# State space stage of a hybrid decoder step: loads one step in front, and keys, values and masks kept in DRAM meanwhile

## The chip, the cores and the metric

One core of a Trainium2 chip runs the whole step in one launch. The metric is the device time of an execution in microseconds; the kernel before took 1545.85 us as the median of three runs (1544.7 to 1550.76). The core's engines are TensorE (PE, weight loads PEld), VectorE (DVE), ScalarE (ACT), GpSimd (POOL) and SyncE (SP), which issues nearly all DMAs.

## The reference

One decoder layer for two groups of requests that share the weights: a prompt of 16 + 512 tokens, and 8 sequences of 8 new tokens each with 1024 cached positions.

```python
u = rmsnorm(h, norm1_w)
z, xbc, dt_raw, q, k, v, qi, ki, wi, g_ssm, g_attn = split_in(u @ w_in)
y_ssm, ssm_new, conv_new = ssm_mixer(z, xbc, dt_raw, ...)      # causal conv, chunked scan, gated norm
y_att = attend(q, k, v, qi, wi, ki)                            # indexer picks 128 (prompt), 256 (sample) keys
merged = sigmoid(g_ssm) * (y_ssm @ w_ssm_proj) + sigmoid(g_attn) * (y_att @ w_attn_proj)
h = h + merged @ w_out
h = h + square(relu(rmsnorm(h, norm2_w) @ w_up)) @ w_down
```

The scan of one chunk (128 tokens; 32 heads of 64 in 4 groups, state of 128) is

```python
acum = cumsum(dc * a_h);  decay = exp(where(causal, acum_i - acum_j, -inf))
y = (cc @ bc.T * decay) @ xdt + (cc @ h.T) * exp(acum)
h = h * exp(last) + (exp(last - acum) * xdt).T @ bc
```

## The kernel before

All is float32. A weight tile of 128 columns is loaded into `wr` (two buffers), cut into a high part `wh` by ScalarE (L128) and a rest `wl` by GpSimd (L129), and a product is three matmuls (`mm3`, L146 to L151).

The stages follow each other in the program. First the input norm, the indexer, keys, values and queries. Keys stay in the tile `KT`, values in `Vt`, the masks of the chosen keys in `am`, all of the pool `ap` (L166 to L170), from there to the end of the attention: 4,736 + 6,144 + 5,376 bytes of each partition. Then the state space stage (L618 to L825), with pools `p3` and `p3s` above them. Then 16 gate tiles (L828), the sampled attention (`sample`, L848), the prompt attention (`query`, L952) interleaved with the product of the state space output (L1036), and the rest of the layer.

In the state space stage two pipes run side by side. The conv pipe takes, for each of four groups, six conv tiles and four `z` tiles: each is a product of 48 matmuls, an evacuation by ScalarE (`rb`, L572 to L575), VectorE work, and stores to DRAM (`d_z`, `d_x`, `d_b`, `d_bc`, `d_xd`). The scan pipe takes, for each group, four `states` units (the sampled sequences: 512 KB of state in, 512 KB out) and five `chunk` units (chunk 4, the sampled tokens, and then 0 to 3), which read back what the conv pipe stored for that group. `start(g)` loads what a group shares (`BT`, `CT`, `xt4`, `Bm`, `xb`, `Bb`). Each push of a pipe lets every live unit, the oldest first, go on to its next `yield`. In the loop of L815 to L824 a push of the scan pipe for group g takes turns with a push of the conv pipe for group g + 1.

`states` loads `st` (two buffers), transposes it, multiplies, adds and stores it again. `chunk` loads `xt`, `Bt` (three buffers), `sz`, `xd`, `EB` (two) and the decay rows `bc` (two tiles a chunk, four buffers), then does the relu and the exponent of `bc` on ScalarE (L729 to L731) and the product `cb` on TensorE, all ahead of its first `yield`. Behind it come eight VectorE products into `bc` (L741), the matmuls with them (L743), the state update and the sum `y`; then the norm, with `rd` (two buffers, as `cb`).

The order in which an engine gets its instructions is not that of the program. The kernel is built with `schedule_with_timeline_sim=True`: a planner follows its own estimate of durations and gives an engine, of the instructions that are ready by that estimate, the earliest one in the program; a load is ready when its tile has a free buffer and its source is there. The result is fixed at build time, and each engine, SyncE's queue too, then goes through its list in order. In the trace the first loads of `st` are issued at 170.81 us and the first conv results of that stage's first group come later.

Of the kernel before, what the change touches and what calls it, by code (L numbers as in the profile page):

```python
# [9 lines left out]
FT = mybir.dt.float32  # L10
# [9 lines left out]
NT, NQ = 592, 576  # L20
# [50 lines left out]
def body(ctx, tc, a, o):  # L71
    nc = tc.nc
    SB, PS, DR = bass.MemoryType.SB, bass.MemoryType.PSUM, bass.MemoryType.DRAM
    act, dve, pool, pe, sy = nc.scalar, nc.vector, nc.gpsimd, nc.tensor, nc.sync
# [5 lines left out]
    drp = ctx.enter_context(tc.tile_pool(name="drp", bufs=1, space=DR))  # L80
# [3 lines left out]
    def pst(tag):  # L84
        return psp.tile([128, 512], FT, tag=tag, name=tag, bufs=PSB[tag])
# [28 lines left out]
    def flat(t):  # L114
        return t.rearrange("p a b -> p (a b)")
# [50 lines left out]
    a_stack = ctx.enter_context(ExitStack())  # L166
    ap_ = a_stack.enter_context(tc.tile_pool(name="ap", bufs=1))
    KT = ap_.tile([128, 2, NT], FT, name="KT")
    Vt = ap_.tile([128, 6, 256], FT, name="Vt")
    am = ap_.tile([128, 1344], FT, name="am")  # L170
# [19 lines left out]
    for t in range(5):  # L190
        xt = p0.tile([128, D], FT, tag="xt", name="xt", bufs=5)
# [12 lines left out]
    for t in range(5):  # L204
        n = 128 if t < 4 else 80
        xt = xts[t]
# [50 lines left out]
    d_xd = drp.tile([16, 128, NT], FT, name="d_xd")  # L257
    d_wi = drp.tile([8, 8, 8], FT, name="d_wi")
    d_ms = drp.tile([128, 1088], FT, name="d_ms")

    def inproj(parts, n=HT, w=None):
        w = w or weights(parts)
        out = []
        for h in range(2):
            ps = pst("w")
            mm3(ps, w, uh, ul, h * n, h * n + n)
            out.append(ps)
        return out
# [25 lines left out]
    with tc.tile_pool(name="p1", bufs=1) as p1:  # L294
# [222 lines left out]
                sy.dma_start(dst[c0:c0 + n] if kt < 5 else os_[0].rearrange("b s h c -> (b s) (h c)"), src)  # L517


        for kp in range(8):  # L520
            hp, gi = divmod(kp, 4)
            parts = []
            for e in range(2):
                c0 = C_Q + 64 * (8 * hp + 4 * e + gi)
                parts.append((lambda r, e=e: r[:, :, 64 * e:64 * e + 64],
                              w_in[:, c0:c0 + 64].rearrange("(k p) c -> p k c", p=128)))
            ps = inproj(parts, n=HQ)
            qs = pf.tile([128, 619], FT, tag="fr", name="qs", bufs=3)[:, :NQ]
            plain(qs, ps, HQ)
            sy.dma_start(d_q[kp], qs)  # L530

    def top_s():
        m8 = pf.tile([128, 8], FT, name="m8s")
# [84 lines left out]
    with tc.tile_pool(name="p3", bufs=1, reuse_waits="tile") as p3, \  # L618
# [42 lines left out]
            G.yi4 = p3s.tile([128, 4, 64], FT, tag="yi4", name="yi4", bufs=1)  # L661

        def load_c(g, c):
            xt = p3.tile([128, 512], FT, tag="xt", name="xt", bufs=3)
            Bt = p3.tile([128, 128], FT, tag="Bt", name="Bt", bufs=3)
            sy.dma_start(xt, d_x[128 * c:128 * c + 128, 512 * g:512 * g + 512])
            sy.dma_start(Bt, d_b[128 * c:128 * c + 128, 128 * g:128 * g + 128])
            return xt, Bt
# [2 lines left out]
            pool.tensor_tensor(h8(dst[:n]), h8(xt[:n]), bc8(v[0][:n, v[1], 8 * g:8 * g + 8], n), op=OP.mult)  # L671

        def states(g, i):
            st = p3s.tile([128, 8, 128], FT, tag="st", name="st", bufs=2)
            r0 = 512 * g + 128 * i
            sy.dma_start(st, a["state_ssm"][0].rearrange("b h p n -> (h p) b n")[r0:r0 + 128])
            sT = p3s.tile([128, 8, 128], FT, tag="sT", name="sT", bufs=1)
            for q in range(2):
                pt_ = pst("a")
                pv = pt_.rearrange("p (k n) -> p k n", k=4)  # L680
                for b in range(4):
                    pe.transpose(pv[:, b, :], st[:, 4 * q + b, :], idf)
                end = act.copy(sT[:, 4 * q:4 * q + 4, :], pv)
            pool.tensor_tensor(st, st, elc[:, 4 * g + i, :, None].to_broadcast([128, 8, 128]), op=OP.mult)
            xr, Bz, CT, yi4 = G.xr, G.Bz, G.CT, G.yi4
            yield
            pj = pst("a")
            for b in range(8):
                q, r = divmod(b, 4)
                mm = pe.matmul(pj[32 * r:32 * r + 32, 128 * q:128 * q + 128], CT[:, 8 * b:8 * b + 32], sT[:, b, :],  # L690
                               start=True, stop=True)
                if b == 0:
                    together(mm, [end])
            yo = p3s.tile([128, 2, 128], FT, tag="yo", name="yo", bufs=2)
            act.copy(yo, pj[:, 0:256].rearrange("p (q n) -> p q n", q=2))
            for q in range(2):
                pn = pst("s")
                pe.matmul(pn, xr[:, q, 128 * i:128 * i + 128], Bz[:, q], start=True, stop=True)
                sv = st[:, 4 * q:4 * q + 4, :].rearrange("p b n -> p (b n)")
                dve.tensor_tensor(sv, sv, pn, op=OP.add)  # L700
            sy.dma_start(o[10][0].rearrange("b h p n -> (h p) b n")[r0:r0 + 128], st)
            yield
            ps = pst("a")
            for q in range(2):
                pe.transpose(ps[:, 128 * q:128 * q + 128], yo[:, q, :], idf)
            act.copy(yi4[:, i, :].rearrange("p (b s) -> p b s", s=8),
                     ps[:, 0:256].rearrange("p (b x) -> p b x", x=32)[:, :, 0:8])

        def chunk(g, c):
# [3 lines left out]
            BT, CT, yi4 = G.BT, G.CT, G.yi4  # L713
            xt, Bt = load_c(g, c) if c < 4 else (G.xt4, None)
            g4 = slice(4 * g, 4 * g + 4)
            sz, xd, EB = [p3.tile([128, 4, 128], FT, tag=x, name=x, bufs=2) for x in ("sz", "xd", "EB")]
            sy.dma_start(sz[:, :, :n], d_z[g4, :, 128 * c:128 * c + n].rearrange("k p n -> p k n"))
            sy.dma_start(xd[:, :, :n], d_xd[g4, :, c0:c0 + n].rearrange("k p n -> p k n"))
            for e in range(2):
# [1 line left out]
                sy.dma_start(EB[64 * e:64 * e + 64, :, :n], src[None].to_broadcast([64, 4, n]))  # L721
            bcs = []
            for q in range(2):
                bc = p3.tile([128, 4, 128], FT, tag="bc", name="bc", bufs=4)
                bcs.append(bc)
                h0 = 8 * g + 4 * q
                sy.dma_start(bc[:n, :, :n], d_ac[None, h0:h0 + 4, 128 * c:128 * c + n].to_broadcast([n, 4, n]))
                for i in range(4):
                    act.activation(bc[:n, i, :n], bc[:n, i, :n], AF.Relu, scale=-1.0,  # L729
                                   bias=acum[:n, c, h0 + i:h0 + i + 1])  # L730
                act.activation(bc[:n, :, :n], bc[:n, :, :n], AF.Exp, scale=-1.0)  # L731
            msk = tri if c < 4 else K("tri4")
            ps = pst("a")
            pe.matmul(ps[:n, :n], BT[:, c0:c0 + n], CT[:, c0:c0 + n], start=True, stop=True)
            cb = p3.tile([128, 128], FT, tag="cb", name="cb", bufs=2)
            dve.tensor_tensor(cb[:n, :n], ps[:n, :n], msk[:n, :n], op=OP.mult)
            yield
            py = pst("s")
# [43 lines left out]
            pe.matmul(ps[:n, 0:1], sq[:, 0, :n], K("ones")[:, 0:1], start=True, stop=True)  # L782
            ss = p3.tile([128, 1], FT, tag="ss", name="ss", bufs=2)
            rstd_of(ss[:n], ps[:n, 0:1], 512, 1, n)
            rd = p3.tile([128, 128], FT, tag="rd", name="rd", bufs=2)
            dve.tensor_scalar(rd[:n, :n], idf[:n, :n], ss[:n], None, op0=OP.mult)
            yield
            rr = pst("a")
# [46 lines left out]
    yp = y_stack.enter_context(tc.tile_pool(name="yp", bufs=1, reuse_waits="tile", side="right"))  # L835
    yah = yp.tile([128, 8, NQ], FR, name="yah")
    yal = yp.tile([128, 8, NQ], FR, name="yal")
    with tc.tile_pool(name="p2s", bufs=1, reuse_waits="tile") as p2, \
            tc.tile_pool(name="p2k", bufs=1, reuse_waits="tile") as p2k:
        qTs = p2.tile([128, 8, 64], FT, name="qTs")  # L840
# [441 lines left out]
```

## Time and profile before

| | us |
|---|---|
| median of three runs | 1545.85 |
| the profiled execution | 1541.95 |
| its span | 1540.2 |
| its mean granted clock, of full speed | 0.985 |
| TensorE busy in the span | 1428.6 |

The profile gives one execution. "Busy" of an engine is the time in which it has an instruction under way; matmuls overlap, so a busy TensorE may still not be at its peak. A wait is the idle time of an engine before an instruction, put down to what released it last. The chain of waits follows the last instruction back through what released it.

### The profile page before, as it was taken

The page shows a single profiled execution, that of the slowest core. Times are in us where ns is not written, and L with a number is a line of the kernel's source. Part 1 is how long each engine was busy: PE and PEld are TensorE (multiplying, and loading weights), DVE is VectorE, ACT ScalarE, POOL GpSimd, SP SyncE. Part 2 cuts the span into 40 slices and gives each one's busy share as a digit, 9 for nine tenths or more (in the row PEclk, how much of TensorE's full clock was granted, in tenths as well). Part 3 has the DMA queues.
Part 4 walks back from the last instruction along what each step waited for, and adds up shares of the span by engine and source line. Part 5 has one row for each costly group of instructions (what it writes and reads, how often), then busy time and mean ns, then how long its engine had stood idle before and what let it go on. Part 6 is the DMA issues. An engine that isn't in the chain of part 4 may idle for free.

```text
span 1540.2 us, 26573 instructions
## 1 busy us (share of the span) xinstructions
PE 1428.6 (93%) x9960; PEld 1290.4 (84%) x9960; DVE 1004.8 (65%) x1905; ACT 664.1 (43%) x1484; POOL 715.4 (46%) x644
## 2 busy tenths in 40 slices
PE   6899999888888898889899999989998999999998
PEld 6888989878878888779788887887897998899886
DVE  5799999878768676461444788864565644564444
ACT  4463445455555465443565565522342321232211
POOL 3422343647656566555445765244254533352322
PEclk9999999999999999999999999999999999999999
DMA  6424555786876877867984432035233312332212
GB/s 184 105 56 112 165 150 149 222 228 168 239 212 186 240 210 182 246 174 213 314 264 156 142 100 79 17 121 178 62 96 110 110 56 69 96 96 67 71 41 69
DMA packets 297609, 221.55 MB, mean 144 GB/s; under 512 B 43820, under 2 KB 267360, under 8 KB 297456
## 3 DMA queue, kind: packets, MB, share of 16 engines
q1 hardware_dynamic: 292232, 200.98, 46.1%
q0 software_dynamic: 5248, 18.88, 3.5%
q8 instruction: 78, 1.28, 0.3%
q14 instruction: 51, 0.42, 0.1%
HBM read 174.97 MB, written 44.07 MB: 142 GB/s over the span
## 4 chain that ended last, share of the span: by engine, by line
PE 51%; DVE 19%; DMA 13%; issue 6%; ACT 6%; POOL 4%; SPq 2%; POOLq 0%; DVEq 0%; ACTq 0%
PE s L1194 13%; PE w L151 12%; PE a L151 10%; PE w L1057 5%; DMA bc<-d_ac 3%; DVE ca L588 2%; DMA wr<-in_w_up_dram 2%; POOL wl L129 2%; DVE scs L536 2%; DVE m8s L535 2%; DVE bc L741 1%; DVE r L1218 1%; ACT wh L128 1%; DVE am L365 1%; DMA d_x<-tk 1%
## 5 line engine op out<-in xcount | busy, mean ns | idle before, releaser
L129 POOL TENSOR_TENSOR wl<-wr,wh 128x1024 fp32r<-128x1024 f32 x128 | 312.1, 2438 | 335.1 <-ACT wh L128 311.5
L151 PE MATMUL w<-uh,wh 128*128 128x288 f32 (+1 forms) x1168 | 360.6, 309 | 21.6 <-ACT rb L572 7.4
L151 PE MATMUL w<-ul,wh 128*128 128x288 f32 (+1 forms) x1168 | 355.7, 305 | 0.6 <-DVE ul L220 0.6
L151 PE MATMUL w<-uh,wl 128*128 128x288 f32 (+1 forms) x1168 | 355.0, 304 | 0.0
L151 PEld LDWEIGHTS w<-uh,wh 128*128 128x128 f32 x1168 | 224.8, 192 | 30.0 <-ACT rb L572 8.6
L151 PEld LDWEIGHTS w<-ul,wh 128*128 128x128 f32 x1168 | 224.9, 193 | 4.5 <-issue 2.9
L151 PEld LDWEIGHTS w<-uh,wl 128*128 128x128 f32 x1168 | 223.6, 191 | 2.1 <-issue 1.4
L128 ACT ACTIVATE wh<-wr 128x1024 fp32r<-128x1024 f32 x129 | 136.2, 1056 | 115.3 <-PE w L151 55.5
L129 POOL TENSOR_TENSOR dl<-wr,dh 128x1024 fp32r<-128x1024 f32 x40 | 99.0, 2477 | 158.1 <-ACT dh L128 157.9
L151 PE MATMUL a<-u2h,wh 128*128 128x288 f32 (+2 forms) x512 | 151.5, 296 | 1.0 <-ACT r L1217 1.0
L151 PE MATMUL a<-u2l,wh 128*128 128x288 f32 (+2 forms) x512 | 151.2, 296 | 0.0
L151 PE MATMUL a<-u2h,wl 128*128 128x288 f32 (+2 forms) x512 | 151.1, 295 | 0.0
L1196 DVE TENSOR_TENSOR h<-h,s 128x512 f32<-128x512 f32 (+1 forms) x101 | 67.3, 679 | 124.6 <-PE s L1194 124.2
L1194 PE MATMUL s<-dh,hh 128*128 128x512 f32 (+1 forms) x324 | 127.6, 395 | 6.3 <-DVE h L1196 6.3
L1194 PE MATMUL s<-dl,hh 128*128 128x512 f32 (+1 forms) x324 | 127.3, 394 | 0.0
L588 DVE SCALAR_TENSOR_TENSOR ca<-rb,cwT,ca 128x616 f32<-128x616 f32 x72 | 96.0, 1334 | 22.9 <-ACT ca L586 22.4
L1218 DVE TENSOR_TENSOR r<-r 128x288 f32<-128x288 f32 (+2 forms) x64 | 74.4, 1163 | 52.9 <-ACT r L1217 52.9
L128 ACT ACTIVATE dh<-wr 128x1024 fp32r<-128x1024 f32 x40 | 42.3, 1058 | 152.3 <-PE s L1194 131.3
L1194 PE MATMUL s<-dh,hl 128*128 128x512 f32 (+1 forms) x260 | 102.5, 394 | 0.0
L151 PEld LDWEIGHTS a<-u2h,wh 128*128 128x128 f32 x512 | 96.1, 188 | 2.1 <-ACT r L1217 1.5
L151 PEld LDWEIGHTS a<-u2l,wh 128*128 128x128 f32 x512 | 96.1, 188 | 0.7
L151 PEld LDWEIGHTS a<-u2h,wl 128*128 128x128 f32 x512 | 96.1, 188 | 0.0
(378 smaller groups left out, 3263.5 us busy)
## 6 DMA issues: line engine op xcount, KB each, us to landing
wr<-in_w_in_dram SPq DMA_DIRECT2D x64, 512.0 KB
wr<-in_w_up_dram SPq DMA_DIRECT2D x32, 512.0 KB
wr<-in_w_down_dram SPq DMA_DIRECT2D x32, 512.0 KB
st<-in_state_ssm_dram SPq DMA_DIRECT2D x16, 512.0 KB
bc<-d_ac SPq DMA_DIRECT2D x32, 256.0 KB
out_dram<-st SPq DMA_DIRECT2D x16, 512.0 KB
wr<-in_w_ssm_proj_dram SPq DMA_DIRECT2D x16, 512.0 KB
d_xd<-th SPq DMA_DIRECT2D x16, 296.0 KB
```

Of the source, the lines that this page charges most:

```text
L128: act.activation(hi, raw, AF.Copy)
L129: (lo_eng or pool).tensor_tensor(lo, raw, hi.bitcast(FT), op=OP.subtract)
L151: pe.matmul(ps[:, :c1 - c0], p[:, k, :], x[:, c0:c1], start=(k == 0 and i == 0), stop=(k == 7 and i == 2))
L365: dve.scalar_tensor_tensor(sc, r[:, :L], wis[:, t, h:h + 1], sc, op0=OP.mult, op1=OP.add)
L535: dve.max(m8, scs)
L536: dve.match_replace(scs, m8, scs, MARK)
L588: dve.scalar_tensor_tensor(ca[:, 0:616], rb[:, k:k + 616], cwT[:, 24 * k + ct:24 * k + ct + 1], ca[:, 0:616], op0=OP.mult, op1=OP.add)
L741: end = dve.scalar_tensor_tensor(mt, mt, dts[:n, c, 8 * g + hh:8 * g + hh + 1], cb[:n, :n], op0=OP.mult, op1=OP.mult)
L1057: pe.matmul(ps[:, :HQ], p[:, k, mc], x[k][:, c0:c1], start=(k == 0 and i == 0), stop=(k == 3 and i == 2))
L1194: pe.matmul(ps, x, w[:, cc], start=(k == 0 and i == 0), stop=(k == len(ws) - 1 and i == len(terms) - 1))
L1196: dve.tensor_tensor(h2[:, t, cc], h2[:, t, cc], ps, op=OP.add)
L1218: dve.tensor_tensor(r, r, r, op=OP.mult)
```

## The change

Three edits go together. The loads of `states` and `chunk` are followed by a `yield` of their own, so that in the program they stand one push ahead of the work on them, and their tiles get one more set of buffers. `rd` takes its buffers from the tag of `cb`, three for both. `KT`, `Vt` and `am` are stored to DRAM when they are complete, their pool is closed ahead of the state space stage, and after the gates they are loaded into a new pool.

```diff
+    d_KT = drp.tile([128, 2 * NT], FT, name="d_KT")
+    d_Vt = drp.tile([128, 6 * 256], FT, name="d_Vt")
+    d_am = drp.tile([128, 1344], FT, name="d_am")
...
+        sy.dma_start(d_KT, flat(KT))
+        sy.dma_start(d_Vt[:, 0:1024], flat(Vt[:, 0:4, :]))
+        sy.dma_start(d_Vt[0:16, 1024:1280], Vt[0:16, 4, :])
+        sy.dma_start(d_Vt[0:64, 1280:1536], Vt[0:64, 5, :])
+        sy.dma_start(d_am, am)
...
+    a_stack.close()
...
         def load_c(g, c):
-            xt = p3.tile([128, 512], FT, tag="xt", name="xt", bufs=3)
-            Bt = p3.tile([128, 128], FT, tag="Bt", name="Bt", bufs=3)
+            xt = p3.tile([128, 512], FT, tag="xt", name="xt", bufs=4)
+            Bt = p3.tile([128, 128], FT, tag="Bt", name="Bt", bufs=4)
...
         def states(g, i):
-            st = p3s.tile([128, 8, 128], FT, tag="st", name="st", bufs=2)
+            st = p3s.tile([128, 8, 128], FT, tag="st", name="st", bufs=3)
             r0 = 512 * g + 128 * i
             sy.dma_start(st, a["state_ssm"][0].rearrange("b h p n -> (h p) b n")[r0:r0 + 128])
+            xr, Bz, CT, yi4 = G.xr, G.Bz, G.CT, G.yi4
+            yield
             sT = p3s.tile([128, 8, 128], FT, tag="sT", name="sT", bufs=1)
...
-            sz, xd, EB = [p3.tile([128, 4, 128], FT, tag=x, name=x, bufs=2) for x in ("sz", "xd", "EB")]
+            sz, xd, EB = [p3.tile([128, 4, 128], FT, tag=x, name=x, bufs=3) for x in ("sz", "xd", "EB")]
...
             for q in range(2):
-                bc = p3.tile([128, 4, 128], FT, tag="bc", name="bc", bufs=4)
+                bc = p3.tile([128, 4, 128], FT, tag="bc", name="bc", bufs=6)
                 bcs.append(bc)
                 h0 = 8 * g + 4 * q
                 sy.dma_start(bc[:n, :, :n], d_ac[None, h0:h0 + 4, 128 * c:128 * c + n].to_broadcast([n, 4, n]))
+            yield
+            for q, bc in enumerate(bcs):
+                h0 = 8 * g + 4 * q
                 for i in range(4):
...
-            cb = p3.tile([128, 128], FT, tag="cb", name="cb", bufs=2)
+            cb = p3.tile([128, 128], FT, tag="cb", name="cb", bufs=3)
...
-            rd = p3.tile([128, 128], FT, tag="rd", name="rd", bufs=2)
+            rd = p3.tile([128, 128], FT, tag="cb", name="rd", bufs=3)
...
+    a_stack = ctx.enter_context(ExitStack())
+    ap_ = a_stack.enter_context(tc.tile_pool(name="ap2", bufs=1, reuse_waits="tile"))
+    KT = ap_.tile([128, 2, NT], FT, name="KT2")
+    Vt = ap_.tile([128, 6, 256], FT, name="Vt2")
+    am = ap_.tile([128, 1344], FT, name="am2")
+    sy.dma_start(flat(KT), d_KT)
+    sy.dma_start(flat(Vt[:, 0:4, :]), d_Vt[:, 0:1024])
+    sy.dma_start(Vt[0:16, 4, :], d_Vt[0:16, 1024:1280])
+    sy.dma_start(Vt[0:64, 5, :], d_Vt[0:64, 1280:1536])
+    sy.dma_start(am, d_am)
```

## Rows read from the trace of the kernel before

**Rows 1.** The page: engine totals, TensorE by slices, the chain by engine.
```profile
PE 1428.6 (93%) x9960; PEld 1290.4 (84%) x9960; DVE 1004.8 (65%) x1905; ACT 664.1 (43%) x1484; POOL 715.4 (46%) x644
...
PE   6899999888888898889899999989998999999998
...
PE 51%; DVE 19%; DMA 13%; issue 6%; ACT 6%; POOL 4%; SPq 2%; POOLq 0%; DVEq 0%; ACTq 0%
PE s L1194 13%; PE w L151 12%; PE a L151 10%; PE w L1057 5%; DMA bc<-d_ac 3%; DVE ca L588 2%; DMA wr<-in_w_up_dram 2%; POOL wl L129 2%; DVE scs L536 2%; DVE m8s L535 2%; DVE bc L741 1%; DVE r L1218 1%; ACT wh L128 1%; DVE am L365 1%; DMA d_x<-tk 1%
```

**Rows 2.** Busy time by windows: length, PE, PEld, DVE, ACT, POOL, clock, DMA share, GB/s.
```profile
180.00:280.00 100.00, 93.69 (x685) 91.22 (x684) 96.61 (x110) 50.27 (x119) 48.31 (x51) 1.00 0.53 147
280.00:410.00 130.00, 113.56 (x866) 103.65 (x865) 99.59 (x153) 70.21 (x171) 80.05 (x80) 0.95 0.75 216
410.00:540.00 130.00, 114.91 (x907) 104.34 (x906) 91.56 (x149) 70.24 (x174) 76.55 (x77) 0.97 0.78 219
540.00:700.00 160.00, 144.30 (x1154) 130.28 (x1154) 98.69 (x211) 78.88 (x191) 94.90 (x84) 0.99 0.74 200
```

**Rows 3.** Two windows inside that stage with a lower granted clock.
```profile
320.00:340.00 20.00, 16.77 (x123) 14.21 (x125) 17.13 (x36) 8.59 (x22) 9.32 (x11) 0.91 0.84 232
500.00:560.00 60.00, 53.70 (x420) 49.42 (x421) 42.90 (x61) 31.64 (x76) 35.00 (x32) 0.91 0.78 226
```

**Rows 4.** TensorE's waits, 280 to 700 us: total us, times, longest.
```profile
PE a L682 <- DMA st<-in_state_ssm_dram: 8.1, 5, 3.5
PE a L782 <- POOL xd L778: 5.0, 5, 1.4
PE s L698 <- DVE xr L656: 4.8, 2, 3.4
PE w L151 <- ACT rb L572: 4.7, 2, 4.2
PE w L151 <- ACT rb L575: 4.4, 2, 2.4
PE s L743 <- DVE bc L741: 4.1, 5, 1.6
PE s L743 <- issue: 4.0, 4, 1.7
PE a L789 <- DVE rd L786: 3.3, 4, 1.9
```

**Rows 5.** Timelines of PE, SyncE's queue and ACT: start, us, instruction, idle before.
```profile
331.21 1.97 PE L743 MATMUL s<-bc,xt 128*64 128x128 f32 x16 [1.69 <-issue]
...
334.35 1.11 SPq L727 DMA_DIRECT2D bc<-d_ac  x2
...
339.92 2.45 ACT L729 ACTIVATE bc<-bc,acum 128x128 f32<-128x128 f32 x8 [3.85 <-DMA bc<-d_ac]
...
497.75 1.28 ACT L729 ACTIVATE bc<-bc,acum 128x128 f32<-128x128 f32 x4 [2.83 <-DMA bc<-d_ac]
...
501.10 0.40 PE L151 MATMUL w<-uh,wh 128*128 128x288 f32 x1 [2.44 <-ACT rb L575]
```

**Rows 6.** ScalarE's waits, 280 to 700 us.
```profile
ACT bc L729 <- DMA bc<-d_ac: 54.4, 19, 9.8
...
ACT Bs L655 <- DMA Bb<-d_b: 16.5, 3, 7.9
```

**Rows 7.** Waits of SyncE's queue, 280 to 700 us.
```profile
SPq L676 <- DMA out_dram<-st: 23.7, 11, 3.8
```

**Rows 8.** Instructions on the tile `am`: count, ns, first and last start.
```profile
L429 DVE TENSOR_TENSOR am<-am,cst x4: 261/270/274, 125.8 to 173.2; 128x128 f32<-128x128 f32 x4
```

**Rows 9.** A window with the cache loads, and the gates' stores by tile.
```profile
720.00:740.00 20.00, 18.22 (x139) 18.01 (x138) 1.17 (x1) 6.12 (x17) 9.20 (x7) 1.00 0.97 318
L553 SPq DMA_DIRECT2D d_g<-tg x16: 332/333/1162, 613.6 to 740.1; - x16
```

**Rows 10.** The chain in order of time, 420 to 430 us: start, us, what.
```profile
423.05 4.08 DMA Bb<-d_b
```

More of the change, by code (lines that the diff above doesn't have):

```diff
@@ L684, in states @@
             pool.tensor_tensor(st, st, elc[:, 4 * g + i, :, None].to_broadcast([128, 8, 128]), op=OP.mult)
-            xr, Bz, CT, yi4 = G.xr, G.Bz, G.CT, G.yi4
             yield
```

## The prediction

> **What bounds the kernel now.** I read the page first. TensorE is busy 93% of the span and its slices read 8 tenths, not 9, nearly throughout from the eighth to the twentieth (270 to 770 us), while the chain that ended last spends only half of itself on TensorE, 13% in DMA, and names the load of `bc` among its lines [rows 1]. So the loss lies in the state space stage, and I cut that stage into windows [rows 2]. From 180 to 280 us VectorE is full (96.61 of 100 us) and no load matters. From 280 to 700 us TensorE works 113.56 + 114.91 + 144.30 = 372.77 of 420 us: 47.2 us are idle, VectorE is at about 70% and the DMA share is 0.74 to 0.78. No engine is full there; the reader is to see a stage in which TensorE, the fullest engine, waits for late neighbours. The granted clock is below 1 in places: 0.91 from 320 to 340 us and over 500 to 560 us [rows 3].
>
> The waits of TensorE in those 420 us say who is late [rows 4]. I sort them by what feeds them. States: 8.1 us for the load of `st`, five times. Chunks: 5.0 (`xd`, L778), 4.1 (`bc`, L741), 4.0 ("issue" ahead of the products of L743) and 3.3 (`rd`), 16.4 us, the steps of a chunk behind its loads. Conv: the 4.4 us behind `rb` L575 belong to the loads too, since ScalarE works in order: a `bc` exponent waited 2.83 us for its load, and TensorE then waited 2.44 us for a copy that stands behind it [rows 5]. Not fed by the moved loads are `xr` 4.8, `rb` L572 4.7 and a rest of 47.2 - 38.4 = 8.8 us. Load-fed: 8.1 + 16.4 + 4.4 = 28.9 us of 47.2.
>
> Are these loads late because of their buffers? One chunk's products at 331.21 us free two `bc` buffers; the loads into them are issued at 334.35, and ScalarE, idle for 3.85 us, starts on them at 339.92 [rows 5]. Four buffers are two chunks, so a load leaves as soon as a buffer is free, and that is too late. Over the stage ScalarE waits 54.4 us for `bc` in 19 waits, 9.8 at the longest [rows 6]. For `st`, with two buffers, SyncE itself stands 23.7 us in 11 waits for the store that empties one [rows 7].
>
> **The change part by part.** The sum is made against the profiled execution, 1541.95 us around a span of 1540.2; the median of the runs is 1545.85, 3.9 us more, and that is added at the end.
>
> The new `yield` as such. Issue order is a planner's, and loads already leave when a buffer is free. So the early place in the program matters through the third set of buffers (`st` 2 to 3, `bc` 4 to 6, `sz`, `xd`, `EB` 2 to 3, `xt`, `Bt` 3 to 4). What it buys is one step: 420 us over 4 groups of 9 pushes is 11.7 us, more than the longest wait of 9.8 [rows 6].
>
> State loads: with a third buffer the load need not wait for the last store but one. Between 0 and 8.1 us [rows 4]; I take 6, since no single wait passes 3.5 us and a step is 11.7.
>
> Chunk loads: between 0 and 16.4 + 4.4 = 20.8 us [rows 4]. Once the load is there, the next to be late is the order on VectorE and GpSimd (L741, then `y`, `xd`, `rd`), which the change leaves alone, so I take a little over half, 12.
>
> Clock: 0.09 of 20 us and 0.09 of 60 us are 1.8 + 5.4 = 7.2 us of full speed lost [rows 3], both stretches with load-fed gaps in them. Between 0 and 7.2; half, 3.5.
>
> Stores of keys, values and masks: 606,208 + 606,208 + 688,128 bytes, 1.90 MB in five DMAs. The mask is the last to be ready, at 173.5 us [rows 8]; its 0.69 MB at the 147 GB/s of the next stage [rows 2] are 4.7 us. Behind it on SyncE's queue are weight loads, two of which can be in flight, and the first `EB` and `bc`, whose products wait for the conv tiles of their group. TensorE is 94% busy in that stage with VectorE as its limit, so I take 0, with 4.7 as the cost if the cover fails. The space of these tiles goes to the stage's first tiles, which are filled only by conv products.
>
> Reloads: 1.90 MB at 318 GB/s [rows 9] are 6.0 us of DMA, in or ahead of the stretch where the cache rows are fetched at a share of 0.97. The space they go to is that of `BT`, `CT` and `xt`, free before the stage's end. Gates, written until 740.1 us [rows 9], keep TensorE fed meanwhile. Between 0 and 6.0; I take 1.5.
>
> The longer pipe, and `rd` sharing three buffers with `cb` where each had two: a step more to drain is covered by the gates, but `rd` can now wait behind a chunk that ran ahead. Between a gain of as much as the `rd` waits now cost and twice that in loss: -3.3 to +6.6 [rows 4]; I take +3.
>
> Loads further in front also stand ahead of others. In the trace a 16 KB piece of `Bb`, which a group's start needs, took 4.08 us from issue to landing [rows 10], when larger transfers were under way. The Trainium skill, "DMA: Bandwidth & Descriptors", section "Queues, rings and completion order", says that what SyncE issues goes through one row of rings and that descriptors are consumed in ring order. By that rule the extra loads would come out ahead of the small ones at a start; what this would make of the time is the second rival below. The row agrees that a small load is slow there, but not why.
>
> Sum: -6 - 12 - 3.5 + 0 + 1.5 + 3 = -17, so 1525 for the profiled execution and 1529 as a median.
>
> **The rivals.** (a) Everything fed by loads closes and the clock stays up: -28.9 - 7.2 = -36.1, 1506, as a median 1510. For it: the loads are a full step early. Against it: the engines between the load and TensorE are 70% busy and in order. (b) A group's start pays. A third `st` (512 KB), and `bc` and `EB` of a third chunk (768 KB), 1.28 MB that no conv product holds back, and with `sz`, `xd` and `xt` 2.05 MB, stand before `Bb` and `xb` of the next group. At 219 GB/s [rows 2] that is 5.8 to 9.4 us, at three starts up to 28; with the forecast's -17 the end is +11, 1553, as a median 1557. It decides from 17 / 3 = 5.7 us per start. For it: ScalarE already waits 16.5 us in three waits for `Bb` [rows 6]. Against it: the bytes are the same and only leave earlier, and TensorE has conv tiles to do at a start. (c) The change doesn't do what it says: the loads leave earlier and land no earlier, since the 16 engines are three quarters busy and SyncE's queue stands in its other waits. Then half of `st`, -4, against +6 of reload and +3: +5, 1547, as a median 1551. For it: 5.6 us from issue to use for one `bc`, when nothing else could hold ScalarE [rows 5]. Against it: that issue came 3 us after the buffer was free.
>
> **How the numbers follow.** Forecast 0.56, (a) 0.10, (b) 0.13, (c) 0.21. The forecast's own range is 1518 to 1541. About 0.5%, 7.7 us, is what a measurement can tell here, so faster means below 1538 and slower above 1553.5. Faster: all of (a) and 0.49 of the forecast, 0.59. Same: the rest of the forecast, most of (c) and a little of (b), 0.27. Slower: 0.14. The range runs from (a) at 1510 to (c) at 1551.
>
> **What would show it.** Right: ScalarE's waits for `bc` fall from 54.4 to below 20 us, SyncE's waits for the store of `st` to below 8, TensorE's idle time between the first chunk and the end of the scan from 47 to about 29 us, the clock of the chunk stretches at 1, and the reloads landed before the first sample product that reads `KT`. Wrong: waits for `bc` that stay above 40 us ((c)); waits for `Bb` or `xr` that grow by more than 17 us in all ((b)); a new wait of TensorE for `KT` or `Kg` beyond 6 us at the start of the attention; or `rd` among its longest waits.

## The result, and the profile after

The kernel after takes 1562.36 us as a median (1556.17 to 1567.02), the kernel before on the same chip 1546.66 (1544.36 to 1552.64): a ratio of 1.0113, 95% interval [1.0091, 1.0136]. It is slower by 1.1%, some 16 us, where 17 us of gain were forecast. The profiled execution took 1560.51 us, with a span of 1558.7 and a mean granted clock of 0.972.

The page of after, to be read against [rows 1]: TensorE's slices from the eighth on read 9 in a few more places, but the twentieth (740 to 779 us) has fallen to 7, and the granted clock of that slice to 8.

```profile
PE 1441.3 (92%) x9960; PEld 1304.4 (84%) x9960; DVE 997.4 (64%) x1905; ACT 666.4 (43%) x1484; POOL 721.4 (46%) x644
...
PE   6899999889888988998799999998998999999998
...
PEclk9999999999999989999899999998999999999999
...
PE 50%; DVE 21%; DMA 12%; ACT 6%; issue 5%; POOL 3%; SPq 2%; POOLq 0%; DVEq 0%; ACTq 0%
```

Windows of after, columns as in [rows 2], the first three being the scan's:

```profile
280.00:410.00 130.00, 114.33 (x879) 105.20 (x880) 92.47 (x152) 70.89 (x172) 80.74 (x81) 0.94 0.79 223
410.00:540.00 130.00, 116.49 (x925) 106.95 (x924) 90.82 (x154) 73.48 (x181) 82.39 (x77) 0.96 0.77 214
540.00:700.00 160.00, 149.65 (x1162) 135.49 (x1161) 95.80 (x204) 73.20 (x173) 95.36 (x82) 0.96 0.71 193
...
740.00:840.00 100.00, 88.53 (x740) 71.12 (x741) 46.16 (x117) 54.84 (x114) 40.57 (x32) 0.93 0.72 230
840.00:1000.00 160.00, 149.40 (x1097) 134.46 (x1096) 123.76 (x424) 90.88 (x244) 93.36 (x162) 0.98 0.36 101
```

The last two of the kernel before:

```profile
740.00:840.00 100.00, 95.14 (x838) 78.54 (x838) 51.26 (x128) 58.02 (x119) 48.40 (x38) 0.98 0.76 240
840.00:1000.00 160.00, 152.93 (x1124) 134.47 (x1121) 128.10 (x442) 94.01 (x254) 93.08 (x167) 1.00 0.31 90
```

TensorE's idle time from 280 to 700 us fell from 47.2 to 420 - 380.47 = 39.5 us, but at a lower clock: it did 2966 matmuls there, 39 more than before. Its last product of the gates ends at 734.7 us (739.6 before), so the scan and the gates gained 5 of the 17 us. TensorE then waits 6.7 us, as shown below, and the first product of the samples starts at 742.5 (742.9). The store of the last gate, at 740.5 us (740.1 before [rows 9]), hides this gain, since ScalarE's copy for it comes behind the same wait. From 740 to 840 us TensorE does 740 matmuls where it did 838, at a clock of 0.93. The first part of the merge that closes the attention (`mgh`) is written from 1013.5 us on (996.9), and what is behind it takes some 2 us more than before. So two things need an answer: why the scan gained so little, and why the attention lost 17 us.

Waits of TensorE in after, 280 to 700 us, against [rows 4]: the wait for `st` has gone from 8.1 to 1.8, and a new one is at the head.

```profile
PE s L592 <- DVE y L778: 12.0, 2, 6.1
PE a L798 <- POOL xd L794: 5.4, 4, 2.3
PE s L759 <- DVE bc L757: 5.1, 3, 2.0
PE a L620 <- DVE rb L605: 4.5, 1, 4.5
...
PE a L696 <- DMA st<-in_state_ssm_dram: 1.8, 1, 1.8
```

The waits of ScalarE, SyncE's queue and VectorE in the same stretch, against [rows 6, 7]; the last line was 3.9 us in 7 waits before:

```profile
ACT bc L745 <- DMA bc<-d_ac: 47.5, 19, 10.0
...
SPq L688 <- DMA out_dram<-st: 28.8, 10, 5.3
...
DVE rd L802 <- POOL ss L161: 20.2, 14, 2.7
```

What the new line is, timelines of GpSimd, VectorE and TensorE in after show (start, length, instruction, idle before):

```profile
390.06 0.54 POOL L161 TENSOR_TENSOR ss<-ss,cst 128x1 f32<-128x1 f32 x1
390.58 1.04 POOL L683 TENSOR_TENSOR xw<-xt,wdt 128x512 f32<-128x512 f32 x1
391.58 1.89 POOL L698 TENSOR_TENSOR st<-st,elc 128x1024 f32<-128x1024 f32 x1
...
390.64 2.92 DVE L802 TENSOR_SCALAR rd<-cst,ss 128x128 f32<-128x128 f32 x1 [2.73 <-POOL ss L161]
393.48 0.68 DVE L778 TENSOR_TENSOR y<-s,EB 128x512 f32<-128x512 f32 x1
...
394.30 0.38 PE L592 MATMUL s<-cst,r 128*27 128x128 f32 x1 [5.91 <-DVE y L778]
```

VectorE stands at `rd`, since `ss` comes from GpSimd, which has other work ahead of it; `rd` then takes 2.92 us, `y` behind it empties the PSUM tile late, and TensorE idles 5.91 us. The second of the two waits has the same rows, and at the end of both the granted clock is at the lower of its two levels (1.2 GHz), 0.50 from 392 to 398 us and from 505 to 511 us (windows as above):

```profile
502.81 2.91 DVE L802 TENSOR_SCALAR rd<-cst,ss 128x128 f32<-128x128 f32 x1 [2.73 <-POOL ss L161]
...
506.46 0.38 PE L592 MATMUL s<-cst,r 128*27 128x128 f32 x1 [6.05 <-DVE y L778]
...
392.00:398.00 6.00, 3.70 (x16) 3.67 (x17) 5.94 (x8) 2.97 (x9) 3.89 (x3) 0.50 1.04 301
505.00:511.00 6.00, 4.54 (x19) 4.51 (x20) 5.94 (x8) 2.89 (x9) 3.89 (x4) 0.50 0.99 295
```

In the kernel before, `rd` stood among other VectorE work and its `ss` was there in most cases. VectorE's lists, as built, show the difference: in before 4.8 instructions stand between `ss` and its `rd` in the mean of 20, in after 1.0 (none in 10 cases), and in 12 of 20 the next instruction behind `rd` is the `cb` of a later chunk.

At the attention's start the rows of after are these: the chain, SyncE's queue, GpSimd, TensorE, and two windows.

```profile
720.85 17.26 DMA qTs<-d_q
...
750.15 0.53 SPq L888 DMA_DIRECT2D P<-d_ms  x1
750.73 2.23 SPq L1066 DMA_DIRECT2D yw<-d_y  x2
...
751.98 0.94 POOL L885 DMA_INDIRECT Kg<-in_cache_k_dram,idx  x1 [14.60 <-PE s L899]
...
742.49 2.83 PE L907 MATMUL s<-KcT,QZ 128*64 128x512 f32 x6 [6.71 <-ACT KcT L900]
...
740.00:760.00 20.00, 14.80 (x97) 9.95 (x98) 7.49 (x23) 9.54 (x22) 6.13 (x5) 0.75 0.92 286
760.00:780.00 20.00, 15.21 (x118) 10.93 (x117) 9.66 (x26) 10.65 (x22) 7.41 (x8) 0.91 0.84 271
```

The queries `qTs`, issued behind the five reloads, are in flight for 17.26 us (at most 6.3 before: issued at 714.59, in use at 720.89). ScalarE waits 6.86 us for them, with its copies of `KcT` and of the last gate behind, and TensorE waits 6.71 us for `KcT` at the first product of the samples (2.2 before). The state space output product (768 matmuls, L1083; the filler below), which fills TensorE beside the samples, can't start before `yw`, and its first load stands on SyncE's queue behind the fourth load of `P`, which waits for a buffer: 750.73 us, where it was at 741.72. GpSimd stands 14.60 us at a gather of keys, and its first split of `yw` is behind that, at 768.27. Of its matmuls 211 have started by 840 us (264 before). The clock of 0.75 says that TensorE spent half of that window at the lower level.

### The profile page after: what moved, and what is told of

It reads as the page before. It is cut to its first block, busy times and chain, and to the rows that moved or that the text cites. A ratio compares the mean times of both kernels' runs of the same rounds, so it can differ in the third digit from the quotient of the medians.

```text
span 1558.7 us, 26591 instructions
## 1 busy us (share of the span) xinstructions
PE 1441.3 (92%) x9960; PEld 1304.4 (84%) x9960; DVE 997.4 (64%) x1905; ACT 666.4 (43%) x1484; POOL 721.4 (46%) x644
## 3 DMA queue, kind: packets, MB, share of 16 engines
q8 instruction: 78, 1.28, 0.3%
## 4 chain that ended last, share of the span: by engine, by line
PE 50%; DVE 21%; DMA 12%; ACT 6%; issue 5%; POOL 3%; SPq 2%; POOLq 0%; DVEq 0%; ACTq 0%
PE s L1220 15%; PE w L151 12%; PE a L151 9%; PE w L1083 4%; DMA bc<-d_ac 3%; DVE ca L600 2%; POOL wl L129 2%; DVE am L430 2%; DMA wr<-in_w_up_dram 2%; DVE m L429 2%; DVE scs L548 2%; ACT wh L128 1%; DVE m8s L547 1%; DVE am L368 1%; DVE r L1244 1%
## 5 line engine op out<-in xcount | busy, mean ns | idle before, releaser
L129 POOL TENSOR_TENSOR wl<-wr,wh 128x1024 fp32r<-128x1024 f32 x128 | 308.7, 2412 | 349.7 <-ACT wh L128 329.7
L600 DVE SCALAR_TENSOR_TENSOR ca<-rb,cwT,ca 128x616 f32<-128x616 f32 x72 | 99.7, 1385 | 36.2 <-ACT ca L598 35.5
```

Of the source, the lines that this page charges most:

```text
L129: (lo_eng or pool).tensor_tensor(lo, raw, hi.bitcast(FT), op=OP.subtract)
L600: dve.scalar_tensor_tensor(ca[:, 0:616], rb[:, k:k + 616], cwT[:, 24 * k + ct:24 * k + ct + 1], ca[:, 0:616], op0=OP.mult, op1=OP.add)
```

## The experiments

Each ratio is to the kernel before, on the same chip, and is not the quotient of two medians: `spill_only`'s 1561.21 over 1545.61 would be 1.0101. Edits are against after unless another kernel is named. Two theories stood at the start: A, the reload of 1.90 MB at the attention's start is the loss; B, the new buffers and yields are, through the planner's order.

**Parts of the change.** `spill_only` has the stores and reloads alone, `spill_yield` adds the two yields, `spill_bufs` has the new buffers instead of the yields.

```diff
# spill_only: the old numbers of buffers, own tag for rd, both new yields out
-            st = p3s.tile([128, 8, 128], FT, tag="st", name="st", bufs=3)
+            st = p3s.tile([128, 8, 128], FT, tag="st", name="st", bufs=2)
...
-            rd = p3.tile([128, 128], FT, tag="cb", name="rd", bufs=3)
+            rd = p3.tile([128, 128], FT, tag="rd", name="rd", bufs=2)
# spill_yield: the same, yields kept;  spill_bufs: only the yields out
-            yield
             sT = p3s.tile([128, 8, 128], FT, tag="sT", name="sT", bufs=1)
```

> Stores and reloads of keys, values and masks alone; buffers and yields as in the kernel before. Theory A (the loss is made by the reloads at the start of the attention, where 1.90 MB go ahead of the queries and cache rows): 1555 to 1564 us, with the first sample product of the state space product's filler as late as in the changed kernel. Theory B (the loss is made by the new buffers and yields, through the order that the planner writes): 1545 to 1551 us, at most 5 us over the kernel before.

Measured: 1561.21 us, ratio 1.0076 [1.0049, 1.0103].

> As the changed kernel, but every tag of the state space stage has its old number of buffers; the yields and the spill stay. Theory A: within 3 us of the spill alone. Theory B, if the yields carry it: within 4 us of the changed kernel, 1558 to 1566; if the buffers carry it: near the spill alone.

Measured: 1540.76 us, 0.9958 [0.9937, 0.9980].

> As the changed kernel, without the two yields; the third buffers and the spill stay. Theory A: the spill's price less what the buffers bring in the scan, 1545 to 1560. Theory B, if the buffers carry it: 1558 to 1566; if the yields carry it: near the spill alone.

Measured: 1570.60 us, 1.0147 [1.0114, 1.0180].

With the yields and all of the reload the kernel is faster than before, so theory A is out as the whole cause. The yields, worth nothing "as such" in the forecast, are worth some 20 us here; the new buffers cost 20 with the yields, and 9 without them.

**The reload, and the stores.** `reload_late` loads the queries first, then `KT` and the rows of `Vt` that the samples need, and the rest (1.23 MB) behind the samples. `store_only` is the kernel before with the five stores.

```diff
-    sy.dma_start(flat(KT), d_KT)
...
         sy.dma_start(qTs, d_q[:, :, 512:576].rearrange("k p n -> p k n"))
+        sy.dma_start(flat(KT), d_KT)
+        sy.dma_start(Vt[0:64, 5, :], d_Vt[0:64, 1280:1536])
...
         Pipe().run(sample(b) for b in range(8))
+        sy.dma_start(flat(Vt[:, 0:4, :]), d_Vt[:, 0:1024])
+        sy.dma_start(Vt[0:16, 4, :], d_Vt[0:16, 1024:1280])
+        sy.dma_start(am, d_am)
```

> As the changed kernel, but at the start of the attention the queries are loaded first, then only the keys and the 64 value rows that the samples read (0.67 MB); the other values and the masks (1.23 MB) follow the samples in the program. Theory A: at least half of the loss goes, 1545 to 1554. Theory B: it stays, 1557 to 1566.

Measured: 1555.07 us, 1.0063 [1.0039, 1.0088]. The reload's place costs after some 6 to 8 us, which is between the two theories. In the profile TensorE's wait at the first product of the samples falls from 6.71 to 1.35 us.

> The kernel before with the five stores alone; nothing reads the copies, KT, Vt and am stay where they were, so the scan's buffers lie as before, and the program's order at the attention's start is that of before (filler matmuls ahead of the products of samples 0 to 7: 0, 0, 20, 48, 84, 120, 156, 192). Traffic theory (the stores' bytes cost the scan the 66 matmuls that spill_only lacked at 740 us, some 9 us): 1553 to 1557 us. Order theory (what spill_only lost came of another order of the same work): within 3 us of the kernel before, 1543 to 1549 us.

Measured: 1543.62 us, 0.9987 [0.9964, 1.0011]. The stores cost nothing that can be measured.

**The yields alone** (the kernel before with two `yield` lines, no spill, old buffers).

> The two yields alone: no stores, no reloads, no new buffers. Traffic theory: the yields gave 20 us on top of the spill (1561 to 1541), so without the spill they should give about as much on top of the kernel before: 1526 to 1533 us. Order theory: spill_only's loss was of its order and the yields only undid it; the order at the attention is that of before, and the scan gains at most the 5 us of spill_yield: 1538 to 1546 us.

Measured: 1538.88 us, 0.9954 [0.9931, 0.9977]. As `spill_yield`: with the yields in, stores and reloads cost about nothing. The 20 us that they gave on top of `spill_only` undid a loss of that kernel; that its order made the loss fits the time, and is not shown.

**Filler first.** `fill_first` writes the first quarter of the output product ahead of the samples.

```diff
+    for q in range(1):
+        ysh, ysl = [], []
+...
     with tc.tile_pool(name="p2s", bufs=1, reuse_waits="tile") as p2, \
...
-    for q in range(4):
+    for q in range(1, 4):
```

> The kernel after, with the first quarter of the state space stage's output product (192 of 768 matmuls) written ahead of the samples, so that the planner takes it first where it is ready; stores, reloads, buffers and yields as in the change. Its order has 0, 0, 0, 12, 14, 108, 192, 192 filler matmuls ahead of the samples' products (after: 0, 0, 0, 12, 14, 72, 108, 144). Order theory (late filler is the loss): the matmuls done by 840 us rise from 211 towards 250, at 0.25 to 0.3 us each: 1550 to 1556 us. Traffic theory (reloads and a throttled clock at the start): 1559 us or more. Third: the samples' own chain is the path, then putting filler ahead of them costs: over 1566 us.

Measured: 1564.02 us, 1.0121 [1.0095, 1.0148]; in the range of the traffic theory: 235 filler matmuls by 840 us, more than after's 211, and no gain. How much filler stands ahead of the samples doesn't by itself tell the time.

**One new buffer set alone.** `sy_cb` is `spill_yield` with only the shared tag of `cb` and `rd`:

```diff
-            cb = p3.tile([128, 128], FT, tag="cb", name="cb", bufs=2)
+            cb = p3.tile([128, 128], FT, tag="cb", name="cb", bufs=3)
...
-            rd = p3.tile([128, 128], FT, tag="rd", name="rd", bufs=2)
+            rd = p3.tile([128, 128], FT, tag="cb", name="rd", bufs=3)
```

> spill_yield with one of the new buffers alone: cb and rd share a tag of three buffers. Its order has the most filler ahead of the samples of all so far (0, 0, 24, 60, 96, 144, 180, 216; spill_yield 0, 0, 0, 12, 24, 84, 120, 156). Order theory: at or below spill_yield, 1532 to 1541 us. Buffer theory (sharing cb with rd makes the scan's DVE work wait, a part of the 20 us between spill_yield and after): 1545 to 1552 us.

Measured: 1570.17 us, 1.0166 [1.0141, 1.0192]. The shared tag alone turns 0.9958 into 1.0166, some 30 us, beyond both theories. Between the two profiled executions (1562.78 and 1543.07 us) little of it is in the scan: the last product of the gates ends at 739.1 us (737.0 in `spill_yield`), the first product of the samples starts at 748.2 (741.3), and over 12 us are lost behind that.

**The shared tag undone**, all else as in after (`after_cb2`):

```diff
-            cb = p3.tile([128, 128], FT, tag="cb", name="cb", bufs=3)
+            cb = p3.tile([128, 128], FT, tag="cb", name="cb", bufs=2)
...
-            rd = p3.tile([128, 128], FT, tag="cb", name="rd", bufs=3)
+            rd = p3.tile([128, 128], FT, tag="rd", name="rd", bufs=2)
```

> The kernel after with one part undone: cb and rd have their own tags again, two buffers each; all other third buffers, yields, stores and reloads stay. Sharing theory (the shared tag is what costs: alone on top of spill_yield it made 1541 into 1570): 1536 to 1548 us, at or below the kernel before. Buffers theory (any deeper set of buffers costs, the shared tag is one of several): 1555 us or more.

Measured: 1541.00 us, 0.9984 [0.9962, 1.0005]: some 20 us below after. Its windows (columns as above) and waits, 280 to 700 us:

```profile
280.00:410.00 130.00, 118.52 (x920) 108.09 (x921) 100.97 (x159) 72.96 (x177) 81.44 (x83) 0.97 0.82 231
410.00:540.00 130.00, 122.97 (x1010) 111.95 (x1010) 104.06 (x173) 78.16 (x192) 87.05 (x83) 1.00 0.84 235
540.00:700.00 160.00, 152.10 (x1159) 139.24 (x1158) 95.46 (x189) 72.23 (x166) 94.29 (x84) 0.96 0.68 189
700.00:740.00 40.00, 33.91 (x261) 29.77 (x260) 10.87 (x26) 17.33 (x37) 19.75 (x15) 0.96 0.97 313
...
740.00:840.00 100.00, 96.35 (x838) 82.98 (x837) 47.94 (x117) 57.73 (x116) 49.78 (x41) 1.00 0.69 218
840.00:1000.00 160.00, 144.30 (x1029) 125.20 (x1029) 135.56 (x435) 84.43 (x238) 78.82 (x156) 0.98 0.28 80
```

```profile
PE w L151 <- ACT zl L284: 7.4, 5, 2.7
PE a L620 <- DVE rb L605: 5.0, 2, 4.6
PE a L798 <- POOL xd L794: 3.2, 3, 2.0
...
PE a L696 <- DMA st<-in_state_ssm_dram: 0.9, 1, 0.9
...
ACT bc L745 <- DMA bc<-d_ac: 29.1, 15, 4.0
...
SPq L688 <- DMA out_dram<-st: 24.0, 9, 5.1
```

TensorE's idle time in the scan is 420 - 393.59 = 26.4 us, the wait behind `y` has gone from 12.0 to 0.7, the waits for `bc` fall from 54.4 to 29.1 us, and the last gate is stored at 723.3 us. The scan has its 17 us: 740.1 - 723.3 = 16.8.

**Buffers or order?** A tag with two names hands out its buffers in the program's order, so the planner must place `rd` ahead of the next chunks' `cb`. `share5` keeps the tag and gives it five buffers, which leaves every engine's list as in after, row by row. `cb1` has `after_cb2`'s lists with one `cb` buffer.

```diff
# share5
-            cb = p3.tile([128, 128], FT, tag="cb", name="cb", bufs=3)
+            cb = p3.tile([128, 128], FT, tag="cb", name="cb", bufs=5)
...
-            rd = p3.tile([128, 128], FT, tag="cb", name="rd", bufs=3)
+            rd = p3.tile([128, 128], FT, tag="cb", name="rd", bufs=5)
# cb1: after_cb2 with cb at bufs=1
```

> The kernel after with five buffers in the tag that cb and rd share, instead of three. Its instructions stand in after's order on all five engines, row by row; only the buffers differ. Buffer theory (cb and rd wait for each other's readers): the waits go, 1541 to 1548 us as after_cb2. Order theory (one tag for two names binds the planner to take them in turn, and the order that comes out is the loss): within 4 us of after, 1558 to 1566 us.

Measured: 1558.88 us, 1.0084 [1.0055, 1.0113].

> after_cb2 with one buffer for cb instead of two (rd keeps two); its instructions stand in after_cb2's order on all engines, row by row. Order theory: the depth of cb is worth nothing, 1538 to 1545 us. Buffer theory (too few buffers for cb and rd cost): VectorE's cb of the next chunk waits for the eight products of the last; 20 chunks by 1 us or more, and PE behind it: 1555 us or more.

Measured: 1544.25 us, 0.9988 [0.9964, 1.0012].

More buffers in after's order change little, fewer in `after_cb2`'s order cost little: the order is the cause, not a lack of buffers. (In `cb1`'s profiled execution, its slowest at 1552.87 us, the last gate is stored at 735.2 us and not at 723.3, so here only the median says that the cost is small.) The waits of `share5`, 280 to 700 us, are like those of after:

```profile
PE s L592 <- DVE y L778: 10.8, 2, 5.7
...
ACT bc L745 <- DMA bc<-d_ac: 55.9, 18, 12.2
...
DVE rd L802 <- POOL ss L161: 21.0, 15, 4.2
```

Between `ss` and `rd` stand 6.5 VectorE instructions in `after_cb2` (5.9 in `spill_yield`), 0.9 in `sy_cb`, 0.5 in `spill_bufs`, 1.0 in after and `share5`. The tag moves much besides `rd`: 568 of VectorE's 1905 places hold another instruction in after than in `after_cb2`, and 245 of 777 on SyncE's queue. No run moves `rd` alone.

**The attention.** `after_cb2` has 17 us at the scan's end and 4 in the whole. Its first query product starts at 840.36 us (854.15 before), its merge at 994.1 (996.9): 3 of the 17 us are lost up to the queries and 11 in them. `p4_dve` went at the queue of after's start, with a fourth `P` buffer and the splits on VectorE:

```diff
-            P = p2.tile([128, 1088], FT, tag="P", name="P", bufs=3)
+            P = p2.tile([128, 1088], FT, tag="P", name="P", bufs=4)
...
-            split(yw, ysh[-1], ysl[-1], (pool, dve)[k % 2])
+            split(yw, ysh[-1], ysl[-1], dve)
```

> The kernel after with a fourth buffer for the samples' P and with the split of yw always on VectorE: SyncE's fourth P load waits for no buffer, so it can't hold the yw loads behind it, and GpSimd's gathers can't hold the splits. The shared tag stays. Queue theory (the first yw loads are at 750.7 us instead of 741.7 because P stands before them, and that is the loss): yw at 743 us or earlier, more than 240 filler matmuls done by 840 us, 1549 to 1555 us. Order theory (what counts is where the filler's matmuls stand among the samples' on TensorE: 0, 0, 0, 2, 12, 48, 92, 132, later than after's): 1560 us or more though yw comes early.

Measured: 1553.31 us, 1.0067 [1.0041, 1.0094]: some 7 us below after, by the time as the queue theory had it. But neither of its signs came. The first `yw` is at 747.98 us, again right behind a load of `P` (now the fifth); it is 11.1 us behind the store of the last gate, where after has 10.2. And 225 filler matmuls have started by 840 us, not over 240. So the time is no evidence for the queue.

> spill_yield (old buffers, stores, reloads, yields) with the reload order of reload_late: queries first, then KT and the last rows of Vt, the rest of Vt and am behind the samples. If the queries' 17 us in flight behind the reload are on the path here too, the 7 us that this gave on after come off: 1532 to 1537 us. If here other work covers them: 1538 to 1543 us, as spill_yield.

Measured: 1541.01 us, 0.9986 [0.9964, 1.0008].

> after_cb2 with the same order of the reload. Additive: 5 to 7 us below after_cb2. If the reload's place is covered once the filler stands ahead of the samples: within 3 us of after_cb2. Against spill_yield it says what the third buffers without the shared tag are worth: nothing by what the waits for bc and st showed (47.5 and 28.8 us against 54.4 and 23.7), 5 us or more if the chunk loads counted.

Measured: 1539.36 us, 0.9973 [0.9952, 0.9994]. Where the tag is not shared, the place of the reload is worth nothing, or 2 us inside the intervals. In `after_cb2` ScalarE waits for the queries as long as in after (6.79 us), but TensorE has gates to do meanwhile and waits 1.30 us at the first product of the samples.

`cb2_actn` and `b_actn` move half of the scalings of `P` in the queries from VectorE to ScalarE, on `after_cb2` and on the kernel before:

```diff
-                    dve.tensor_scalar(P2[:, e, :128 * nk], P2[:, e, :128 * nk], mx[:, e, 4:5], None, op0=OP.mult)
+                    if e:
+                        act.activation(P2[:, e, :128 * nk], P2[:, e, :128 * nk], AF.Copy, scale=mx[:, e, 4:5])
+                    else:
+                        dve.tensor_scalar(P2[:, e, :128 * nk], P2[:, e, :128 * nk], mx[:, e, 4:5], None, op0=OP.mult)
```

> after_cb2, and in the query stage of the attention half of the scalings of P (64 of 128, some 0.5 us each) on ScalarE instead of VectorE. Theory V (behind 840 us VectorE is the bound, 135.6 us busy of 160, so what the scan gained is lost there): the end of the query stage comes 8 to 14 us earlier, 1527 to 1534 us. Theory F (the query stage is bound by the order, or by TensorE's own work, and the scan's gain was lost before 840 us): within 4 us of after_cb2, 1537 to 1545 us.

Measured: 1535.61 us, 0.9942 [0.9919, 0.9965].

> The kernel before with the same half of the scalings of P on ScalarE. Theory V with TensorE as bound in this kernel's query stage (152.9 us busy of 160 between 840 and 1000 us): at most 5 us, 1540 to 1546 us. If VectorE bounds it here as well: as much as on after_cb2, 1531 to 1538 us, and the move says nothing of where the scan's gain went.

Measured: 1546.37 us, 1.0007 [0.9985, 1.0029].

The move gives 5 us where the scan is early and none where it isn't. The window 840 to 1000 us of `cb2_actn`, against that of `after_cb2`: VectorE 13 us less, TensorE 4 us more.

```profile
840.00:1000.00 160.00, 148.54 (x1067) 130.42 (x1066) 122.48 (x410) 101.12 (x273) 78.06 (x157) 0.98 0.30 86
```

So part of the loss in the queries is VectorE's, about half of what was expected of it. The expectation had counted double: the trace of `after_cb2` has 64 such scalings, with a median of 0.41 us, and `cb2_actn` moves 32 of them.

**The fastest.** `ny_actn` is `nospill_yield` with that move, `late_actn` is `cb2_late` with it.

> nospill_yield with half of the scalings of P on ScalarE. If what a scan's earlier end is worth is lost in the query stage at VectorE, 5 us of an end that is 17 us earlier come back by the move; here the end is 5 us earlier and the time already 6 us lower, so nothing is left to give back: 1536 to 1542 us, as nospill_yield (1539). If the move is worth 5 us wherever the yields are: 1531 to 1535 us.

Measured: 1540.36 us, 0.9966 [0.9941, 0.9991]: nothing to give back there.

> cb2_late with half of the scalings of P on ScalarE. The two steps on after_cb2 were worth 5 us (the move) and 1.6 us (the late reload): additive, 1532 to 1536 us, the fastest so far; if the query stage's order is what holds it, no better than cb2_late, 1537 to 1541 us.

Measured: 1533.63 us (1528.71 to 1540.21), 0.9923 [0.9899, 0.9948], the fastest: all of the change but the shared tag, with the late reload and the move, 0.8% below the kernel before and 29 us below the kernel after.

## Why the prediction was wrong

**The step that failed** is the last of the sum, "`rd` sharing three buffers with `cb`", taken at +3 between -3.3 and +6.6. It was priced as a wait for a buffer, from TensorE's waits for `rd` in [rows 4]. Measured, it is some 20 us (1.0113 to 0.9984), and it is not a wait for a buffer (`share5`): one tag for two names binds the order, `rd` moves up to its `ss`, VectorE waits there 20.2 us for GpSimd, and TensorE behind it. In the profile the price is 39.5 - 26.4 = 13.1 us of idle TensorE in the scan, most of it the wait behind `y` (12.0 us against 0.7), and the clock: 0.94 and 0.96 against 0.97 and 1.00 in the first two windows. The last product of the gates ends 11.9 us later (734.7 against 722.8), and TensorE's wait for the queries, which other work no longer covers, adds 5.4 us at the samples' start (6.71 against 1.30). That the shared tag costs 20 to 30 us, by the order, is shown by adding it, by undoing it and by `share5`. That it costs them by this wait is read from the rows of after and `share5`, and it isn't the whole: in `sy_cb` VectorE waits for `ss` at `rd` too (11.9 us from 280 to 700), yet TensorE's idle time there is 37.7 us against 40.5 in `spill_yield`, and most of the loss lies behind the scan. The rows that could have shown the danger were VectorE's and GpSimd's waits around `ss`; only TensorE's had been read.

**The state loads** (-6): right in the scan. TensorE's waits for `st` went from 8.1 to 1.8 us, to 0.9 in `after_cb2`. The sign that was named for it, SyncE's wait for the store below 8, did not come (28.8 and 24.0): SyncE still stands there, and it no longer matters.

**The chunk loads** (-12): right where the tag is apart, in TensorE's idle time and not in the whole. `bc` waits of 29.1 us against 54.4, not below 20, but TensorE's idle time of 26.4 us is what "47 to about 29" said. The yields alone bring it to 35.9 us, so about half of the fall is the third buffers', which in time gave nothing: 0.9984 with them (`after_cb2`), 0.9958 without (`spill_yield`). In after the waits stay at 47.5, above the 40 that was the sign of rival (c). Yet (c) isn't what happened: with the same loads, yields and buffers the waits fall as soon as `rd` is out of the way.

**The yield as such**: wrong. It was to matter only through the third buffers; alone it gives 0.9954, and TensorE's idle time of 280 to 700 us falls from 47.2 to 35.9. The planner takes the earliest instruction in the program among the ready ones, and two lines further up change what that is.

**The clock** (-3.5): wrong on after. The two stretches that were named rose, that of 320 to 340 us [rows 3] from 0.91 to 1.00, that of 500 to 560 us from 0.91 to 0.94 (0.97 in `after_cb2`). But others fell, and the stage as a whole is at 0.94, 0.96 and 0.96 against 0.95, 0.97 and 0.99 [rows 2]: by the prediction's own count, share times length, 7.4 us more are lost. `after_cb2` gains 1.7 by that count.

**The stores** (0): right, `store_only`.

**The reloads** (+1.5): too small on after, where moving them gave 6 to 8 us, and about right where the tag is apart. The gates kept TensorE fed until 734.7 us in after, but what came next needed `qTs`, which stood behind 1.90 MB. The sign named for this, a wait of TensorE beyond 6 us at the start of the attention, came with 6.71 us, for the queries and not for `KT`. The Trainium skill, "DMA: Bandwidth & Descriptors", section "Queues, rings and completion order", says that on each engine of one issuer's rings descriptors are consumed in ring order; the 17.26 us of that small load agree. The ring need not be the whole of it: in those 17.26 us SyncE's queue moved 3.03 MB, and GpSimd's gathers of cache rows 3.15 MB beside it.

**What the sum left out**: it took what the scan gains as gained. Of the 16.8 us of `after_cb2` 14 are lost in the attention. Two rows carry 12.9 of them: 40 - 33.91 = 6.1 us of idle TensorE from 700 to 740 us against 1.8 before, and 15.7 against 7.1 from 840 to 1000 us, where VectorE is busy 135.56 us of 160 and beside the queries less of the filler is left (370 of 768 matmuls have started by 840 us). In after the attention took 17 us more from a start that was not earlier. Which part of that is the reload, which the queue at `P`, and which the rest of the new order is not settled; `fill_first` and `p4_dve` don't add up to one account. Nor is it settled why `spill_only`, which differs from `store_only` by the closed pool and the reload, loses 1.0076 against 0.9987 while `rd` stands where it stood before.

**The sign for `rd`**, that it would be among TensorE's longest waits, did not come: the wait is VectorE's, and TensorE's is put down to `y`.

**Rival (b)** had no part: TensorE's wait for `xr` is 3.3 us against 4.8, and no `Bb` wait grew. Two of the prediction's readings were a little off, and nothing hung on them. Its 1.28 and 2.05 MB, counted in KB of 1,024 bytes, are 1.31 and 2.10 MB. And its 3 us from a free `bc` buffer to the issue run from the products' start; they end at 333.18 us [rows 5], 1.2 us ahead of the issue.

## What to carry to other kernels

Where a planner fixes the order, a tag shared by two tiles is a constraint on the order before it is a saving of space: two names in one ring are taken in the program's turn, and an engine that works in order then waits in place for the later one's input. To tell a wait for buffers from an order, give the ring more buffers and see that the lists stay the same, as in `share5`. And a gain in one stage is a gain in the whole only if the next stage can start on it: look at what bounds that stage when it comes early.

## What the hardware showed that was not expected

A VectorE instruction can last as long as GpSimd's next ones. `rd` has a median of 0.287 us in after and took 2.92 at 390.64 us, from 0.06 us after the start of two GpSimd products to 0.09 us after the end of the second; at 502.81 us it took 2.91 beside the same two. In `after_cb2` a split of `yw` on VectorE, 0.76 us at 859.87, took 5.32:

```profile
843.90 5.32 DVE L129 TENSOR_TENSOR ysl<-yw,ysh 128x576 fp32r<-128x576 f32 x1
...
842.23 2.71 POOL L1001 TENSOR_TENSOR QS<-R,QS 64x512 fp32r<-64x512 f32 x2
844.90 1.40 POOL L129 TENSOR_TENSOR ysl<-yw,ysh 128x576 fp32r<-128x576 f32 x1
846.27 2.33 POOL L129 TENSOR_TENSOR wl<-wr,wh 128x1024 fp32r<-128x1024 f32 x1
```

The Trainium skill, "SBUF — State Buffer", section "SBUF: two separate sides", says that VectorE and GpSimd share a pair of ports as an exclusive lock, which a VectorE instruction needs in a two-port mode or with two inputs in SBUF: the one that comes second is blocked for the whole instruction. The rows agree (the split has two such inputs; the mode of `rd` no row tells), and they go further: here VectorE did not get in between GpSimd's instructions that followed each other without a gap. It isn't always so. Another `rd` of after started 0.06 us after the start of a GpSimd product (691.37 to 691.83 us) and ended 0.07 us after its end, though GpSimd's next had begun without a gap:

```profile
691.43 0.47 DVE L802 TENSOR_SCALAR rd<-cst,ss 128x128 f32<-128x128 f32 x1 [1.96 <-POOL ss L161]
...
691.78 2.39 POOL L129 TENSOR_TENSOR wl<-wr,wh 128x1024 fp32r<-128x1024 f32 x1
```
